# Extra matmuls behind the last product of an encoder layer: 640 with set operand places, results unread

## The chip, the cores and the metric

The kernel runs on one core of one Trainium2 chip. A core has TensorE (matrix products, called PE in the profile, with its weight loads as PEld), VectorE (DVE), ScalarE (ACT), GpSimd (POOL) and SyncE (SP), which here mostly issues DMAs. The engines run side by side and meet through semaphores. Operands of a product lie in SBUF, an on-chip memory of 128 partitions; results go to PSUM, the accumulators of TensorE, in buffers of 512 columns of four bytes. The metric is the time of one execution in microseconds, as the device measures it; lower is better.

## The reference

One step of a one-layer hybrid encoder: 1024 prompt frames and 64 frames of a running stream, width 1024. The last part is the one that the change stands behind:

```python
x = x + m                                   # m: the merged convolution and attention branches
x = x + swiglu(rmsnorm(x, g_ffn[l]), w_ff1[l], w_ff3[l], w_ff2[l])
...
return rmsnorm(x, g_final), ...

def swiglu(x, w1, w3, w2):
    return (jax.nn.silu(x @ w1) * (x @ w3)) @ w2
```

The hidden width of the feed-forward part is 2816. Besides the two normalised outputs, the step returns key and value rows and the states of the convolution.

## The kernel before

All large products run on TensorE in the type fp32r. Each float32 operand is split into a high part and a low part (`split`, line 119: ScalarE copies the high part, VectorE subtracts), and a product is made of three matmuls: high by high, high by low, low by high. A matmul `mm(out, stationary, moving)` loads 128 columns of weights (the stationary operand) and streams the moving operand, here 272 or 512 columns, past them. Products of 2 x 2 blocks are made by a scheme of seven products instead of eight (`STEPS`, line 126), with sums of blocks prepared by VectorE.

The order of work on TensorE is the order in which the code calls it: input projections and attention first, then the gates and output projection (lines 294 to 302 and 1066 to 1068), then the two upward products of the feed-forward part, written by `run` (line 218, its matmuls at line 238, 272 columns each, 24 in a group), and at last the downward product (lines 1461 to 1553).

The downward product takes 11 blocks of the hidden width, in four runs of 2, 3, 3 and 3 (`KB`, line 35). For each run, each of two groups of frames and each of the seven steps, it accumulates into a PSUM tile at line 1508, with 512 columns to a matmul. The hidden values come from HBM as the tiles `ht`. The weights of the downward product stand in rings in SBUF: `ring_of(p)` (line 1266) gives, for each of the seven steps p, one tile of 128 partitions by 4352 fp32r columns; block kp uses columns (kp mod 4) x 1024 onwards, high part first, low part 512 columns later. Columns from 4096 on hold other operands. Columns 3072 to 3583 of ring 1 also serve ScalarE as a place to throw away squares when it sums a row (line 1448).

The PSUM tiles of the downward product come from the pool `psD`: two buffers with the tag "A" and four with the tag "BD". A new tile of a tag takes the oldest buffer of that tag, and waits until its last reader is done. The reader is the add at line 1520, by which VectorE takes each product into an accumulator in SBUF.

In the last run (`final`), the last three steps are done for one frame tile after the other (line 1493). After each of them `half_ended` (line 1443) squares and sums half an output row, and when both halves are there it computes the factor, scales the halves on ScalarE (line 1456) and VectorE (line 1458), and stores them from the queues of ScalarE and SyncE (lines 1457 and 1459). The last matmul of the program is the last one of line 1508. After it only this tail runs, and then the end of the program, in which SyncE waits for every queue and engine in turn and all engines meet (line 1587).

Of the kernel before, what the change touches and what calls it, by code (L numbers as in the profile page):

```python
# [8 lines left out]
F32 = mybir.dt.float32  # L9
# [6 lines left out]
P = 128  # L16
# [48 lines left out]
def encoder_kernel(ctx: ExitStack, tc: tile.TileContext, ins, outs):  # L65
# [1396 lines left out]
    for b, ks in enumerate(blocks):  # L1462
        first, final = b == 0, b == len(blocks) - 1
        nk = blocks[b + 1] if not final else []
        for g in range(2):
# [28 lines left out]
            for si, js in turns:  # L1494
# [47 lines left out]
                if final and g == 0 and si == 4:  # L1542
# [9 lines left out]
                    vec.scalar_tensor_tensor(row, row, r[:TS], gfb[:TS], op0=ALU.mult, op1=ALU.mult)  # L1552
                    nc.sync.dma_start(outs["y_sample"], row)

_OUTS = [
    ("y_prompt", (1024, 1024), (1, 1024, 1024)),
    ("y_sample", (64, 1024), (1, 64, 1024)),
# [33 lines left out]
```

## Time and profile before

| | |
|---|---|
| time, median of two runs | 1512.9 us (1512.77 to 1513.04) |
| span of the profiled execution | 1513.8 us |
| instructions in it | 26451 |
| matmuls, weight loads | 10178 each |
| TensorE, share of the span busy with matmuls | 98% |
| VectorE, ScalarE | 65%, 45% |
| mean granted clock of TensorE | 0.994 |

The profiled execution is 0.9 us longer than the median of the timed runs. The profile gives for each engine its busy time, a picture of the span in 40 slices, groups of instructions with the line that made them, and, in time order, single instructions or runs of equal ones. In such a row come the start, the length, the engine, the line, the operation, the tiles written and read, and the count. A row whose engine ends in q is the engine's queue, which issues DMAs or waits. The chain of waits is followed back from the last instruction; its rows have start, length and what the time went to. Matmuls overlap in the array, so that the lengths of single matmuls add up to more than the time they take together; the step from one start to the next tells the pace.

### The profile page before, as it was taken

The page shows a single profiled execution, that of the slowest core. Times are in us where ns is not written, and L with a number is a line of the kernel's source. Part 1 is how long each engine was busy: PE and PEld are TensorE (multiplying, and loading weights), DVE is VectorE, ACT ScalarE, POOL GpSimd, SP SyncE. Part 2 cuts the span into 40 slices and gives each one's busy share as a digit, 9 for nine tenths or more (in the row PEclk, how much of TensorE's full clock was granted, in tenths as well). Part 3 has the DMA queues.
Part 4 walks back from the last instruction along what each step waited for, and adds up shares of the span by engine and source line. Part 5 has one row for each costly group of instructions (what it writes and reads, how often), then busy time and mean ns, then how long its engine had stood idle before and what let it go on. Part 6 is the DMA issues. An engine that isn't in the chain of part 4 may idle for free.

```text
span 1513.8 us, 26451 instructions
## 1 busy us (share of the span) xinstructions
PE 1476.9 (98%) x10178; PEld 1381.1 (91%) x10178; DVE 981.2 (65%) x1843; ACT 682.7 (45%) x1397; POOL 128.7 (9%) x236
## 2 busy tenths in 40 slices
PE   7999999999999999999999999999999999999997
PEld 5799999999999999998889999999999998788886
DVE  6886465642776752763489667666666668857576
ACT  6654433333776752542256444444444445402123
POOL 1210010001111121000100011100001011000000
PEclk9999999999999999999999999999999999999999
DMA  7597524168676529554432434443334449667675
GB/s 233 181 305 245 184 78 135 57 187 234 181 186 176 151 82 293 164 167 145 140 126 77 143 134 152 144 148 120 117 142 157 143 177 317 234 221 235 222 259 202
DMA packets 167518, 264.73 MB, mean 175 GB/s; under 512 B 19008, under 2 KB 103168, under 8 KB 167264
## 3 DMA queue, kind: packets, MB, share of 16 engines
q1 hardware_dynamic: 146736, 198.23, 42.2%
q0 software_dynamic: 19504, 62.71, 11.4%
q10 hardware_dynamic: 1152, 2.10, 0.4%
q8 instruction: 80, 1.31, 0.4%
q14 instruction: 46, 0.38, 0.1%
HBM read 171.06 MB, written 91.92 MB: 174 GB/s over the span
## 4 chain that ended last, share of the span: by engine, by line
PE 79%; DMA 8%; DVE 6%; ACT 3%; issue 3%; SPq 1%; POOL 0%; ACTq 0%; POOLq 0%; DVEq 0%
PE Aa L238 9%; PE Ab L238 9%; PE A L1508 7%; PE Da L238 4%; PE Db L238 4%; PE D L1508 3%; PE Bb L238 2%; PE Ba L238 2%; PE B L1508 2%; PE wo L1066 2%; PE wo L1068 2%; PE wo L1067 2%; PE t L903 2%; PE Ak L238 2%; PE g L300 2%
## 5 line engine op out<-in xcount | busy, mean ns | idle before, releaser
L1508 PE MATMUL A<-ring,ht 128*128 128x512 f32 x528 | 126.6, 393 | 3.6 <-ACT acc L1518 1.9
L1508 PEld LDWEIGHTS A<-ring,ht 128*128 128x128 f32 x528 | 98.8, 188 | 27.2 <-ACT acc L1518 3.2
L300 PE MATMUL g<-xn,whp 128*128 128x272 f32 x384 | 113.2, 295 | 0.0
L301 PE MATMUL g<-xn,whp 128*128 128x272 f32 x384 | 112.0, 292 | 0.0
L302 PE MATMUL g<-xn,wlp 128*128 128x272 f32 x384 | 111.6, 291 | 0.0
L121 ACT CAST ring<-w2r 128x512 fp32r<-128x512 f32 (+1 forms) x78 | 43.4, 587 | 105.7 <-PE A L1508 52.6
L121 ACT CAST hq<-sa 128x512 fp32r<-128x512 f32 x77 | 47.7, 619 | 86.4 <-DVE sa L1239 56.6
L814 DVE CUSTOM_DVE_ANT_0 p<-s,bb 128x640 f32<-128x640 f32 (+5 forms) x72 | 47.5, 661 | 45.5 <-DMA bb<-bias_d 28.6
L1227 POOL DMA_DIRECT2D h_d<-hq x77 | 40.9, 532 | 416.5 <-DVE hq L122 242.1
L122 DVE TENSOR_TENSOR hq<-sa,hq 128x512 fp32r<-128x512 f32 x77 | 53.1, 690 | 33.4 <-ACT hq L121 33.3
L300 PEld LDWEIGHTS g<-xn,whp 128*128 128x128 f32 x384 | 72.6, 189 | 1.0
L302 PEld LDWEIGHTS g<-xn,wlp 128*128 128x128 f32 x384 | 72.6, 189 | 0.5
L301 PEld LDWEIGHTS g<-xn,whp 128*128 128x128 f32 x384 | 72.7, 189 | 0.3
L1508 PE MATMUL D<-ring,ht 128*128 128x512 f32 x264 | 63.9, 393 | 1.3 <-ACT acc L1518 1.3
L122 DVE TENSOR_TENSOR wla<-rawa,wha 128x512 fp32r<-128x512 f32 x56 | 38.5, 687 | 40.5 <-ACT wha L121 40.5
L238 PE MATMUL Aa<-tt,wha 128*128 128x272 f32 x352 | 59.1, 289 | 2.5 <-ACT tt L121 2.5
L1508 PEld LDWEIGHTS D<-ring,ht 128*128 128x128 f32 x264 | 49.5, 188 | 13.1 <-ACT acc L1518 1.8
L122 DVE TENSOR_TENSOR ring<-w2r,ring 128x512 fp32r<-128x512 f32 (+1 forms) x78 | 49.0, 647 | 14.4 <-ACT ring L121 14.2
L238 PE MATMUL Ab<-mg,whb 128*128 128x272 f32 x352 | 58.4, 288 | 0.0
L238 PE MATMUL Aa<-mg,wha 128*128 128x272 f32 x352 | 58.3, 288 | 0.0
L238 PE MATMUL Ab<-tt,whb 128*128 128x272 f32 x352 | 58.2, 287 | 0.0
L121 ACT CAST wha<-rawa 128x512 fp32r<-128x512 f32 x56 | 34.8, 621 | 51.3 <-PE Ab L238 35.3
(519 smaller groups left out, 4368.2 us busy)
## 6 DMA issues: line engine op xcount, KB each, us to landing
h_d<-hq POOLq DMA_DIRECT2D x77, 512.0 KB, 3.5
ht<-h_d SPq DMA_DIRECT2D x154, 256.0 KB, 3.7
rawa<-in_w_ff SPq DMA_DIRECT2D x11, 1024.0 KB, 5.9
rawb<-in_w_ff SPq DMA_DIRECT2D x11, 1024.0 KB, 5.4
w2r<-in_w_ff SPq DMA_DIRECT2D x11, 1024.0 KB, 5.8
qd<-q_d SPq DMA_DIRECT2D x32, 272.0 KB, 4.7
rawp<-in_w_in SPq DMA_DIRECT2D x6, 1024.0 KB, 5.9
u_d<-scr SPq DMA_DIRECT2D x8, 544.0 KB, 4.6
```

Of the source, the lines that this page charges most:

```text
L121: act.copy(hi, src)
L122: vec.tensor_tensor(lo, src, hi.bitcast(F32), op=ALU.subtract)
L238: mm(t[:, j, :HN], w[:, k, :], x[p][:, l, k, j * HN : (j + 1) * HN], start=p in (1, 2, 7) and k == 0 and n == 0, stop=k == 3 and n == 2, s ...
L300: mm(out, a, p, start=k == 0, stop=False)
L301: mm(out, a, q, start=False, stop=False)
L302: mm(out, b, p, start=False, stop=k == kt - 1)
L814: vec.tensor_tensor_reduce(out=s if len(ps.shape) == 2 else s.rearrange("p (a b) -> p a b", a=2), in0=ps, in1=bias if len(ps.shape) == 2 e ...
L903: nc.tensor.transpose(tp[:, i * P : (i + 1) * P], s[:, i * P : (i + 1) * P], ident)
L1066: mm(ps, x(k, 0), wh, start=f, stop=False)
L1067: mm(ps, x(k, 0), wl, start=False, stop=False)
L1227: nc.gpsimd.dma_start(h_d[p, c - 1], hq.rearrange("p i l t -> p (i l t)").bitcast(F32))
L1508: mm(t, ht[k][:, j, x], w[:, l], start=p in (1, 2, 7) and k == 0 and n == 0, stop=k == len(ks) - 1 and n == 2, skip_group_check=p in (6, 5 ...
```

## The change

One block of code is added behind the downward product. Nothing else is touched.

```diff
+    for half in range(2):
+        pr = psD.tile([P, 512], F32, tag="A", name=f"pr{half}", bufs=2)
+        pq = psD.tile([P, 512], F32, tag="BD", name=f"pq{half}", bufs=4)
+        mv, st = ring_of(1), ring_of(2)
+
+        def some(n, count, ms, ss, banks=(0,), fresh=False):
+            for c in range(count):
+                a, b = ms[c % len(ms)], ss[c % len(ss)]
+                o = (pr, pq)[banks[c % len(banks)]]
+                mm(o[:, :n], st[:, b : b + P], mv[:, a : a + n], start=fresh or c < 2, stop=fresh or c >= count - 2,
+                   skip_group_check=True)
+
+        if half == 0:
+            for d in range(16):
+                some(272, 14, (128,), (128 + 8 * d,))
+            for d in (0, 16, 32, 64):
+                some(272, 14, (136,), (8 + d,))
+            some(272, 14, (128, 400), (128,))
+            some(272, 14, (128, 512), (128,))
+            some(272, 14, (128, 512), (128, 256))
+            some(272, 14, (128, 400), (128,), banks=(0, 1))
+            some(272, 14, (128, 512), (128,), banks=(0, 1))
+            some(272, 14, (128,), (128,), fresh=True)
+            some(272, 14, (128, 400, 2304, 2576, 128, 400), (128, 128, 128, 128, 2304, 2304), banks=(0, 1))
+            some(256, 14, (128,), (128,))
+            some(256, 14, (128,), (160,))
+            some(256, 14, (128,), (192,))
+            some(288, 14, (128,), (128,))
+            some(320, 14, (128,), (128,))
+        else:
+            for d in (0, 8, 16, 24, 32, 48, 64, 80, 96, 112):
+                some(512, 12, (128,), (128 + d,))
+            some(512, 12, (136,), (8,))
+            some(512, 12, (136,), (136,))
+            some(512, 12, (128,), (256,))
+            some(512, 12, (128, 640), (256,))
+            some(384, 12, (128,), (128,))
+            some(512, 12, (128,), (128,), fresh=True)
```

`some(n, count, ms, ss)` issues `count` matmuls of n columns. Their moving operands start at the columns `ms` of ring 1, in turn, and their weights at the columns `ss` of ring 2, in turn; both rings still hold the weights of the downward product. A set accumulates in one PSUM tile, or in two by turns where `banks` says so; with `fresh` every matmul starts its accumulation anew. Nothing reads `pr` or `pq`, and the outputs are the same as before. There are 448 matmuls in the first half and 192 in the second. Most sets keep both operands at one place throughout, and the sets differ in the distance of the two places (8 columns are 32 bytes), in whether an operand alternates between two places, and in the width.

## The prediction

> **What bounds the kernel now.** I read the head of the page first (span, busy time, granted clock), then TensorE's own rows in time order over the last 30 us, then the chain of waits for the pace of long matmul groups, and last the rows behind the final matmul.
>
> ```profile
> span 1513.8 us, 26451 instructions
> PE 1476.9 (98%) x10178; PEld 1381.1 (91%) x10178; DVE 981.2 (65%) x1843; ACT 682.7 (45%) x1397; POOL 128.7 (9%) x236
> PEclk9999999999999999999999999999999999999999
> ```
>
> TensorE is busy 98% of the span, in every slice but the first and the last, and the clock that it was granted never shows under nine tenths. So TensorE bounds the kernel. Work put behind its last matmul can be hidden by one thing alone: what the kernel still does after that matmul. The rows at the end say how much that is:
>
> ```profile
> 1501.60 2.21 PE L1508 MATMUL D<-ring,ht 128*128 128x512 f32 x9
> 1503.64 2.20 PE L1508 MATMUL A<-ring,ht 128*128 128x512 f32 x9
> ...
> 1499.92 0.67 DVE L1520 TENSOR_TENSOR acc<-A,acc 128x512 f32<-128x512 f32 x1
> 1504.37 0.68 DVE L1520 TENSOR_TENSOR acc<-D,acc 128x512 f32<-128x512 f32 x1
> 1505.98 0.68 DVE L1520 TENSOR_TENSOR acc<-A,acc 128x512 f32<-128x512 f32 x1
> 1509.01 0.75 DVE L1458 SCALAR_TENSOR_TENSOR acc<-acc,n4y,gfb 128x512 f32<-128x512 f32 x1
> 1509.79 0.33 SPq L1459 DMA_DIRECT2D out_y_prompt<-acc  x1
> ...
> L1587 POOLq EVENT_SEMAPHORE x4: 17/17/17, 1513.1 to 1513.7; - x4
> DMA to landing us min/median/max: 2.0/3.3/6.5
> ```
>
> The columns of the first rows are start, length, engine and line; the last two rows are from the views of line 1587 and of the output tensor. The last product ends at 1503.64 + 2.20 = 1505.84 us. Then VectorE adds it up, the last output half is scaled until 1509.76, its store is issued at 1509.79 and lands 2.0 to 3.3 us later, and the closing handshake of the engines runs from about 1513.1 to 1513.8. So 8.0 us of the span lie behind the last matmul, and that is all the cover there is.
>
> **The change part by part.** It removes nothing and moves nothing. It adds 640 matmuls to TensorE, behind everything that TensorE did, in program order: 448 in the first half (27 sets of 14 with 272 columns, three of 256, one of 288, one of 320) and 192 in the second (15 sets of 12 with 512 columns, one of 384). No other engine gets an instruction, no DMA is added, and no queue has anything put in front of what it did. Each matmul brings its own weight load, as each of the 10178 of before does (PEld has the same count).
>
> *Price of one.* TensorE overlaps matmuls, so the mean length in the groups (some 0.29 us for 272 columns, 0.39 for 512) is not what one costs. What it costs is the step from one start to the next, read from long unbroken groups:
>
> ```profile
> 1024.73 2.99 PE Aa L238 x24
> 1027.72 3.00 PE Da L238 x24
> 1030.72 3.01 PE Aa L238 x24
> ...
> 1340.86 4.11 PE D L1508 x18
> 1344.96 8.16 PE A L1508 x36
> 1353.12 4.09 PE B L1508 x18
> 1359.09 4.20 PE A L1508 x18
> ```
>
> These rows of the chain are start, length, count. L238 has 272 columns: 3.00 us / 24 = 125 ns. L1508 has 512: 8.16 / 36 = 227 ns in one place, 4.20 / 18 = 233 ns in another. Shape, type and line are the same there, and only the tiles differ, so the place of the operands is worth about 3% here. Single steps spread further:
>
> ```profile
> 341.78 0.29 PE L300 MATMUL g<-xn,whp 128*128 128x272 f32 x1
> 341.91 0.30 PE L301 MATMUL g<-xn,whp 128*128 128x272 f32 x1
> 342.05 0.28 PE L302 MATMUL g<-xn,wlp 128*128 128x272 f32 x1
> 342.17 0.28 PE L300 MATMUL g<-xn,whp 128*128 128x272 f32 x1
> ...
> 764.99 0.40 PE L1067 MATMUL wo<-wol,mg 128*128 128x512 f32 x1
> 766.14 0.40 PE L1066 MATMUL wo<-woh,mg 128*128 128x512 f32 x1
> 766.38 0.39 PE L1067 MATMUL wo<-wol,mg 128*128 128x512 f32 x1
> 769.85 0.39 PE L1067 MATMUL wo<-wol,mg 128*128 128x512 f32 x1
> ...
> 475.10 0.31 PE L856 MATMUL s<-kd,qd 128*128 128x320 f32 x1
> 475.68 0.49 PE L903 MATMUL t<-ident,p 128*128 128x128 f32 x3
> ```
>
> A 272-column step is 0.14 us (341.91 to 342.05) or 0.12 (342.05 to 342.17), and a 512-column one up to 0.24 (766.14 to 766.38). Between 764.99 and 769.85 lie 21 steps of 512, 231 ns each. Between 475.10 and 475.68 lie four of 320 columns, 145 ns each.
>
> I take 125 ns for 272 columns: three groups in different tiles agree within 1%, and 27 sets of different places should average as those do. For 512 columns I take 231 ns, between 227 and 233 and equal to the third place. From these two the slope is (231 - 125) / 240 = 0.442 ns a column. That gives estimates of 118 ns for 256 columns, 132 for 288 and 174 for 384; 320 has its own 145.
>
> The sum:
> - 272 columns: 378 x 125 ns = 47.3 us
> - 256: 42 x 118 = 5.0; 288: 14 x 132 = 1.8; 320: 14 x 145 = 2.0
> - 512: 180 x 231 = 41.6; 384: 12 x 174 = 2.1
> - together 99.8 us
>
> *Bounds.* With every set at the slow steps (140 ns and 240 ns, the rest 13 ns dearer in the first half and 10 in the second) the sum is 52.9 + 43.2 + 12.0 = 108.1 us. With every set at the slope alone (120 ns for 272, 226 for 512, the others likewise) it is 45.4 + 40.7 + 10.5 = 96.6.
>
> *A rule weighed.* The rows show 125 ns at 272 columns and 227 to 233 at 512. The Trainium skill, "TensorE: Matmul & The Clock Gate", section "Back-to-back issue gap", gives a warm gap of columns / 2.4 plus 2.5 ns, so 116 and 216 ns; by it the sum would be an estimate of 92.8 us and the time about 1598.7. The trace disagrees by 9 and by 11 to 17 ns a matmul, and the trace decides here.
>
> *Waits.* The new accumulators take over PSUM buffers of the last products, so a matmul could wait for VectorE. The first one takes the buffer of the A product before the last, whose last add starts at 1499.92; the second one's kind is read for the last time by 1504.37 + 0.68 = 1505.05. Both are done before TensorE is free at 1505.84. The second half's accumulator waits for the add of 1505.98, done at 1506.66; that half begins 58 us later. I price all three at nothing. If an add were late, TensorE would stand for its 0.7 us. The columns of the ring that ScalarE's squares still write (3072 to 3583) are read by no new matmul.
>
> *The end.* New matmuls follow at the pace of their predecessors, so the last one ends at 1505.84 + 99.8 = 1605.6 us. The old tail (until 1513.8) lies under the first 8 us of them and costs nothing any more. What is late next is TensorE itself; behind it comes only the closing handshake. SyncE waits there for each engine in turn. It took at least 0.7 us (from 1513.1), and at most 2.0 if the last store landed after its least 2.0 us at 1511.8. I take 1.0, near the row that shows it, so the span is 1606.6. The median of the runs, 1512.9, lies 0.9 under the profiled span of 1513.8; I carry that over: 1605.7 us, 92.8 more than before, 6.1%.
>
> **The rivals.**
>
> *The places lock into collisions.* In the kernel before, both operands' places change from matmul to matmul, so a slow step (140 ns, 240 ns) is soon followed by a fast one. A set of the change repeats one pair of places 12 or 14 times; a bad pair would be paid each time. Against it: groups with one kind of place held 233 ns for 18 matmuls and never 240. For it: nothing in the trace repeats the same moving columns at 272 or 512 wide. All sets bad gives 108.1 us and 1614.0; I give it 0.08, since place is worth 6 ns at 512 columns (227 against 233) and nothing forbids 13. The same Trainium skill page, section "Step-by-step: what each phase is for", says that loading the next weights takes no SBUF read bandwidth from the running matmul, since there are two ports. By that, places would not matter; the trace, 227 against 233 ns, does not agree with so flat a rule.
>
> *Repeated operands go at the bare slope.* If what lies above the slope is paid for changing operands, sets that repeat them cost 96.6 us, and the time is 1602.5. Unchanged weights alone do not save it: L238 uses each weight block for two or four matmuls in a row and pays 125 ns. Chance 0.06. The gap that the Trainium skill states, weighed above, would go further the same way.
>
> *The clock falls or the matmuls stop overlapping.* After an idle stretch this kernel shows what the slow clock costs:
>
> ```profile
> 810.82 1.11 PE L238 MATMUL Bb<-mg,whb 128*128 128x272 f32 x4
> 811.73 0.66 PE L238 MATMUL Bb<-mg,wlb 128*128 128x272 f32 x2
> ...
> 1330.00:1500.00 170.00, 170.00 (x749) 1.00 0.71 232
> 1506.00:1513.80 7.80, 0.00 (x0) 0.75 0.36 137
> ```
>
> Four matmuls took 0.91 us, 227 ns each instead of 125. The window rows give length, busy time (count), granted clock and DMA: 1.00 while TensorE works, 0.75 once it is idle. At 227 / 125 of the price the sum is 181 us and the time 1687. TensorE has no gap in front of the new work, so the clock has no reason to fall: 0.03.
>
> *Not slower.* The results are unread; if the program did not keep these matmuls, or kept them under the 8 us tail, the time would stay 1512.9. Within 2% means at most 30.3 us more: 640 matmuls would have to cost under 60 ns each with the tail's 8 us, less than half the 125 ns of a row. All 640 stand in the built program behind the last product, each with its wide output, and even TensorE's idle 36.9 us (1513.8 - 1476.9), if all were filled, would leave 63 of the 99.8. That the change does nothing gets 0.01.
>
> **How the numbers follow.** The forecast holds 0.82 and gives 1605.7; locked collisions 0.08 (1614), bare slope 0.06 (1602.5), slow clock 0.03 (1687), nothing done 0.01 (1512.9). The range takes in the bounds of the pace, 1602.5 to 1614.0. It goes on by 1 us above for a longer closing, and by 2.5 below for a shorter closing (0.3) and for the 68 matmuls whose width has no row of its own (some 30 ns each is 2 us): 1600 to 1615. Slow clock and nothing done stay outside. About 2% is what a measurement tells from no change: slower 0.99, same 0.01, faster 0.
>
> **What would show it right or wrong.** The page of the changed kernel should have 10818 matmuls and as many weight loads, and every other engine as before. A new line with 640 matmuls should start within 0.3 us of the last L1508 one and run without a gap for about 100 us; the last two of 40 slices should be TensorE alone, with the clock at nine tenths or more. Its 272-column sets should step at 120 to 130 ns, those of 512 at 226 to 235. The chain should end on TensorE, with about 1 us behind it. A gap in front, a set far above its neighbours, or a clock under 0.9 would prove a step wrong.

## The result and the profile after

The changed kernel took 1609.0 us (two runs, 1607.15 and 1610.85) against 1512.9 us: a ratio of 1.0623, 95% interval 1.0587 to 1.0658. It is slower by 6%, as forecast (1605.7), and inside the range.

The page of the changed kernel begins with the span, TensorE's busy time and, among the 40 slices (now 40 us each), TensorE, VectorE and the granted clock:

```profile
span 1605.1 us, 27731 instructions
PE 1574.2 (98%) x10818; PEld 1469.9 (92%) x10818; DVE 982.2 (61%) x1843; ACT 683.6 (43%) x1397; POOL 128.7 (8%) x236
PE   7999999999999999999999999999999999999999
DVE  6885465616777527635886666666666875767400
PEclk9999999999999999999999999999999999999999
```

There are 640 more matmuls and as many weight loads; VectorE, ScalarE and GpSimd have the counts of before. The last two slices are TensorE alone, at full clock. In order of time, TensorE's rows around the new work (start, length, count) are these. The gap holds 41 rows with the other 55 matmuls; the last row covers several widths and carries the form of its first matmul:

```profile
1501.91 2.20 PE L1508 MATMUL A<-ring,ht 128*128 128x512 f32 x9
1503.95 40.79 PE L1564 MATMUL pr<-ring,ring 128*128 128x272 f32 x323
...
1551.49 52.60 PE L1564 MATMUL pr<-ring,ring 128*128 128x256 f32 x262
```

The last old product ends at 1501.91 + 2.20 = 1504.11; the first new one has started 0.16 us before, since matmuls overlap. The last one ends at 1551.49 + 52.60 = 1604.09. So the new work moves TensorE's end by 100.0 us, and 1.0 us of the span lies behind it. Cut at the second half (the second window stops at 1604.00, 0.09 us short of the last end), the windows (length, busy time of TensorE, weight loads, VectorE, ScalarE, GpSimd, then clock, DMA share, GB/s) are:

```profile
1503.95:1560.39 56.44, 56.44 (x450) 56.44 (x448) 3.43 (x11) 2.60 (x8) 0.00 (x0) 1.00 0.06 22
1560.39:1604.00 43.61, 43.61 (x194) 35.74 (x192) 0.00 (x0) 0.00 (x0) 0.00 (x0) 1.00 0.00 0
```

The rows of SyncE's waits from 1500 us on say what the change cost the kernel, since SyncE ends the program (waited in total, times, longest):

```profile
SPq L1626 <- PE pr L1564: 93.0, 1, 93.0
SPq L1626 <- DMA out_y_prompt<-acc: 2.1, 2, 1.7
```

In the kernel before, SyncE's longest wait at that point is this one, and it has none for a matmul:

```profile
SPq L1587 <- DMA out_y_prompt<-acc: 2.3, 3, 1.7
```

Now SyncE waits for the last stores much as before, and then 93.0 us for TensorE. That wait ends with TensorE at 1604.1, so it began about 1511.1, which is 7.0 us behind the last old product.

### The profile page after: what moved, and what is told of

Read it like the earlier page. It is cut to its first block, busy times and chain, and to the rows that moved or that the text cites. A ratio compares the mean times of both kernels' runs of the same rounds, so it can differ in the third digit from the quotient of the medians.

```text
span 1605.1 us, 27731 instructions
## 1 busy us (share of the span) xinstructions
PE 1574.2 (98%) x10818; PEld 1469.9 (92%) x10818; DVE 982.2 (61%) x1843; ACT 683.6 (43%) x1397; POOL 128.7 (8%) x236
## 4 chain that ended last, share of the span: by engine, by line
PE 63%; issue 25%; DMA 4%; DVE 3%; POOL 2%; ACT 2%; SPq 1%; POOLq 0%; ACTq 0%; DVEq 0%
PE A L1508 7%; PE pr L1564 6%; PE Ab L238 5%; PE Aa L238 5%; PE D L1508 3%; PE Db L238 3%; PE Da L238 2%; PE B L1508 2%; PE t L903 2%; PE Ak L238 2%; PE Acc L238 1%; PE Acb L238 1%; PE Ach L238 1%; PE g L300 1%; PE g L301 1%
## 5 line engine op out<-in xcount | busy, mean ns | idle before, releaser
L1564 PE MATMUL pr<-ring,ring 128*128 128x272 f32 (+5 forms) x619 | 100.1, 320 | 0.0
L1564 PEld LDWEIGHTS pr<-ring,ring 128*128 128x128 f32 x619 | 91.0, 188 | 7.6
L121 ACT CAST hq<-sa 128x512 fp32r<-128x512 f32 x77 | 47.7, 619 | 87.1 <-DVE sa L1239 56.4
```

The lines of the kernel that those rows point to most:

```text
L121: act.copy(hi, src)
L1564: mm(o[:, :n], st[:, b : b + P], mv[:, a : a + n], start=fresh or c < 2, stop=fresh or c >= count - 2, skip_group_check=True)
```

## The experiments

The first two tell apart whether TensorE's end decides or whether each matmul is paid from the first. Line 1560 is the new line there. Nothing else is left out or changed in these two kernels.

**26 matmuls.**

```diff
-    for half in range(2):
-...
+    pr = psD.tile([P, 512], F32, tag="A", name="pr", bufs=2)
+    mv, st = ring_of(1), ring_of(2)
+
+    def some(n, count, a, b, m=P):
+        for c in range(count):
+            mm(pr[:m, :n], st[:, b : b + m], mv[:, a : a + n], start=c < 2, stop=c >= count - 2, skip_group_check=True)
+
+    some(512, 26, 128, 192)
```

> The added block is replaced by one set of 26 matmuls of 512 columns, both operands at one place each (moving at column 128 of ring 1, weights at column 192 of ring 2). Theory (TensorE's end decides, the old tail covers what fits beneath it): 26 x 227 ns = 5.9 us, TensorE ends about 1511.7 on the old clock, before SyncE gets to wait for it near 1512.8, so the time is that of before, within 0.3%. Rival (the matmuls disturb the tail, or every one is paid from the first): 5.9 us more, 0.4%.

Measured: ratio 1.0009, interval 0.9992 to 1.0026: no difference, though TensorE works 6 us longer; the rival's 0.4% lies outside the interval. SyncE's waits from 1508 us on hold no wait for `pr`.

**62 matmuls.** The last line is `some(512, 62, 128, 192)`.

> The same with 62 matmuls: 62 x 227 ns = 14.1 us. Theory: TensorE ends 14.1 us behind the last product, about 8.0 us of it lie beneath the old tail and about 1.0 us of closing comes behind, so about 7.1 us more than before (0.47%). Rival (every matmul paid from the first): 14.1 us more (0.93%).

Measured: ratio 1.0048, interval 1.003 to 1.0066, which is 7.3 us (4.5 to 10.0); 14.1 us would be 1.0093. The trace of this kernel, TensorE's row and SyncE's wait:

```profile
1503.98 14.21 PE L1560 MATMUL pr<-ring,ring 128*128 128x512 f32 x62
...
SPq L1596 <- PE pr L1560: 7.1, 1, 7.1
```

Half of the 14.1 us lies beneath the tail, and the other half is SyncE's wait. The rival is out.

**The change again, with more runs.**

> The changed kernel once more, against before, in more rounds, because two runs of each leave the size of the step open. Theory (matmuls cost their step, the tail covers 8.0 us of them, 1.0 us of closing follows): 99.8 - 8.0 + 1.0 = 92.8 us more than the median of before on the same chip, a ratio of 1.061. Rival (the 96.1 us that the two runs showed are the true size, so some 3 us come from a cost that the sum leaves out): a ratio of 1.0635.

Measured: 1608.6 us against 1515.6 us (17 runs of before, from 1511.4 to 1519.3), ratio 1.0614, interval 1.059 to 1.0638: 93.0 us between the medians. The theory's 1.061 lies in the middle of the interval, the rival's 1.0635 just inside its upper edge, so the times alone favour the theory and don't rule the rival out. The trace leaves it little room: in this profile too SyncE waits 93.0 us for `pr`, and TensorE's end moves by the 100.0 us that the sum has as 99.8.

**The same matmuls ahead of the last run of the downward product.**

```diff
         nk = blocks[b + 1] if not final else []
+        if final:
+            for half in range(2):
+                pr = psD.tile([P, 512], F32, tag="A", name=f"pr{half}", bufs=2)
+...
```

> The same 640 matmuls, put ahead of the last of the four runs of the downward product instead of behind it. Theory: no tail lies beside them there, and the old tail and closing stay at the end, so the time grows by the whole 99.8 us, 7.0 us more than with the changed kernel (0.43%); VectorE, ScalarE and the DMAs, which get 100 us ahead, win nothing back, since TensorE bounds what follows without a gap. Rival (the other engines use the time to clear waits of TensorE in the last run, or the cover was not there): the same time as the changed kernel, within 2 us, or below it.

Measured: 1614.3 us, ratio 1.0653, interval 1.0634 to 1.0672. That is 5.8 us above the changed kernel by the medians, where 7.0 was expected; the profiled spans are 1614.3 and 1607.6. TensorE's last row and the last row of VectorE:

```profile
1604.12 2.20 PE L1547 MATMUL A<-ring,ht 128*128 128x512 f32 x9
...
1609.49 0.75 DVE L1458 SCALAR_TENSOR_TENSOR acc<-acc,n4y,gfb 128x512 f32<-128x512 f32 x1
```

TensorE ends at 1606.32 and the span at 1614.3: the old tail of 8.0 us is back behind it, uncovered. The rival is out: the fastest of the five runs (1613.4) lies above the slowest of the changed kernel (1613.0). The two intervals just overlap, so the runs don't settle the size (5.8 or 7.0). The trace does: the added matmuls take 100.0 us (1444.15 to 1544.13), and from the first product of the last run to TensorE's end it is 1606.32 - 1544.13 = 62.2 us, as in the kernel before (1505.84 - 1443.65). So nothing was won back, and the whole difference is the tail of 8.0 us in place of the closing of 1.0.

The kernels of the next two experiments and of the last two ran once each, at granted clocks of 0.996 to 0.998. What they show is read from the starts of matmuls in that one trace.

**Long sets at many distances.** The change has 12 or 14 matmuls to a set, too few to see every set settle. The edit is shown against the kernel with 26 matmuls.

```diff
-    some(512, 26, 128, 192)
+    for n in (512, 272):
+        for d in (64, 72, 80, 88, 96, 104, 112, 120):
+            some(n, 40, 128, 128 + d)
```

> The added block is replaced by 16 long sets of 40 matmuls with both operands fixed: moving at column 128, weights at 192, 200, 208, 216, 224, 232, 240, 248; first 512 columns wide, then 272. Theory (the distance of the two places, by 64 columns or 256 bytes, sets a settled pace, small against the whole): after some ten steps each set settles; 512 wide at 227 for distance 64, about 233 for 72, 80, 88 and 104, 232 for 96 and 120, 229 for 112; 272 wide at 124 to 127; sum 320 x 231 + 320 x 126 = 114 us, span about 1621. Rival (bad places lock into collisions): at least one set stays at 240 or more at 512, or 135 or more at 272, for all 40 steps. Rival (history, not place): the settled pace of a set depends on the set ahead of it and neighbours do not differ.

The rows of the sets, in order; the step is the difference of two neighbouring starts, divided by 40. The first three are 512 wide at distances 64, 72 and 80, then come 104 and 112, the row behind them is distance 120, and the last five are 272 wide at 64, 72, 80, 88 and 96:

```profile
1507.70 9.24 PE L1560 MATMUL pr<-ring,ring 128*128 128x512 f32 x40
1516.77 9.49 PE L1560 MATMUL pr<-ring,ring 128*128 128x512 f32 x40
1526.10 9.50 PE L1560 MATMUL pr<-ring,ring 128*128 128x512 f32 x40
...
1554.08 9.50 PE L1560 MATMUL pr<-ring,ring 128*128 128x512 f32 x40
1563.41 9.33 PE L1560 MATMUL pr<-ring,ring 128*128 128x512 f32 x40
1572.59 9.49 PE L1560 MATMUL pr<-ring,ring 128*128 128x512 f32 x40
1581.91 5.17 PE L1560 MATMUL pr<-ring,ring 128*128 128x272 f32 x40
1586.92 5.22 PE L1560 MATMUL pr<-ring,ring 128*128 128x272 f32 x40
1591.98 5.10 PE L1560 MATMUL pr<-ring,ring 128*128 128x272 f32 x40
1596.92 5.13 PE L1560 MATMUL pr<-ring,ring 128*128 128x272 f32 x40
1601.89 5.22 PE L1560 MATMUL pr<-ring,ring 128*128 128x272 f32 x40
```

At 512 columns distance 64 steps by (1516.77 - 1507.70) / 40 = 227 ns and distance 72 by (1526.10 - 1516.77) / 40 = 233. At 272, distance 80 steps by (1596.92 - 1591.98) / 40 = 123.5 ns and distance 72 by 126.5. No set stays at 240 or 135: collisions don't lock. Neighbours differ, so place does count, and by 3% at most. What is cheap at one width isn't at the other. The paces came as expected within about 1 ns, and the span was 1623.2 us where about 1621 was.

**Fewer weight columns.** With 96, 64 or 32 weight columns, only so many rows of the product are computed. These lines stand in place of `some(512, 26, 128, 192)`.

```diff
+    for b in (192, 144):
+        for m in (128, 96, 64, 32):
+            some(512, 40, 128, b, m)
+    for a, b in ((136, 200), (136, 152), (144, 208), (144, 160)):
+        some(512, 40, a, b)
```

> The added block is replaced by 12 sets of 40 matmuls of 512 columns. Sets 1 to 4: moving at 128, weights at 192 (distance 64), with 128, 96, 64 and 32 weight columns; sets 5 to 8: the same with weights at 144 (distance 16); sets 9 to 12: 128 weight columns, moving and weights at (136, 200), (136, 152), (144, 208), (144, 160). Theory (the weight load of the next matmul and the moving stream get into each other's way in reading SBUF): at distance 64 all four at 227; at distance 16 the pace falls from 233 with 128 weight columns towards 227 with 32, by about 1.6 ns per 32 columns; and what counts is the distance, so sets 9 and 11 settle at 227, 10 and 12 at 233. Rival (the place of the moving operand alone decides): the number of weight columns changes nothing at distance 16, and sets 9 and 10 agree, as do 11 and 12.

The rows: distance 64 with 128, 96, 64 and 32 weight columns, distance 16 with the same, and the last four:

```profile
1507.45 9.23 PE L1560 MATMUL pr<-ring,ring 128*128 128x512 f32 x40
1516.53 9.37 PE L1560 MATMUL pr<-ring,ring 128*96 128x512 f32 x40
1525.73 9.35 PE L1560 MATMUL pr<-ring,ring 128*64 128x512 f32 x40
1534.92 9.43 PE L1560 MATMUL pr<-ring,ring 128*32 128x512 f32 x40
1544.19 9.49 PE L1560 MATMUL pr<-ring,ring 128*128 128x512 f32 x40
1553.52 9.30 PE L1560 MATMUL pr<-ring,ring 128*96 128x512 f32 x40
1562.66 9.47 PE L1560 MATMUL pr<-ring,ring 128*64 128x512 f32 x40
1571.96 9.43 PE L1560 MATMUL pr<-ring,ring 128*32 128x512 f32 x40
1581.23 9.28 PE L1560 MATMUL pr<-ring,ring 128*128 128x512 f32 x40
1590.35 9.50 PE L1560 MATMUL pr<-ring,ring 128*128 128x512 f32 x40
1599.68 9.28 PE L1560 MATMUL pr<-ring,ring 128*128 128x512 f32 x40
1608.80 9.49 PE L1560 MATMUL pr<-ring,ring 128*128 128x512 f32 x40
```

The part on distance holds: with the moving operand 32 and 64 bytes further on, the sets at distance 64 take 9.28 us and those at 16 take 9.50 and 9.49, so it is the distance that counts, not the place of one operand. (Weights at column 200 step by (1590.35 - 1581.23) / 40 = 228 ns here, with the moving operand at 136, and stepped by 233 above, with it at 128.) The part on the weight load falls. At distance 64 fewer weights make a set slower (9.23 to 9.43), at distance 16 they go 9.49, 9.30, 9.47, 9.43. With 32 weight columns both distances take 9.43. That fits a distance that counts through the weight load, but it is one pair of distances, and a shorter load is no cheaper; how the load acts is not shown.

**32 bytes of padding in the kernel before.** Nothing is added to TensorE.

```diff
     tpool = ctx.enter_context(tc.tile_pool(name="tpool", bufs=1, reuse_waits="tile"))
+    vec.memset(tpool.tile([P, 8], F32, name="pad"), 0.0)
```

> The kernel before with 32 bytes put ahead of the tiles of the pool that holds the rings of the steps 6, 7 and 5, so that these rings stand at the same distance to the tiles of hidden values (by 256 bytes) as the rings of the steps 1 to 4; no matmul is added. Theory (distance sets the pace): the 396 matmuls of 512 columns of these steps go from 233 to 227 ns, 2.6 us less; the 1584 matmuls of 272 columns that read the same place in the upward products move too, from 124.5 to about 125.5 ns, up to 1.6 us more; the time falls by about 1 us, which a measurement can hardly tell from nothing, and the trace shows the steps. Rival (these rings are slower for another reason, such as the side of SBUF that they stand on): the steps stay at 233 ns.

Measured: ratio 1.0003, interval 0.9991 to 1.0015. Rows of its chain of waits, downward product first:

```profile
1360.71 4.08 PE A L1509 x18
1364.80 4.08 PE D L1509 x18
...
1002.66 3.01 PE Db L238 x24
1020.70 3.01 PE Aa L238 x24
```

The groups that took 4.20 us before take 4.08 (227 ns a step), and groups of the upward product that took 2.99 take 3.01. Both moved as the distance says, and the rival is out. From its first matmul to its last the downward product takes 1505.47 - 1267.08 = 238.4 us, against 1505.84 - 1264.34 = 241.5 before. The time shows nothing: an expected gain of about 1 us lies inside the interval, which goes from 1.4 us less to 2.3 more. That the gain and the loss in the upward products cancel is worked out from the steps and not seen in the time. It is no better kernel.

**Operands of two bytes.** VectorE copies 2048 columns of each ring into a bf16 tile `two` (`raw` in the code), and the sets read that tile; four sets in fp32r stand ahead. The lines that make the copy and define `some` with 40 matmuls to a set are left out here.

```diff
+...
+    for n in (512, 272):
+        for d in (64, 80):
+            some(ring_of(1), ring_of(2), n, 128, 128 + d)
+    for n in (512, 272):
+        for d in (0, 32, 64, 16):
+            some(raw, raw, n, 128, 2304 + d)
```

> The added block is replaced by 12 sets of 40 matmuls: four in fp32r as in the change (512 columns at the distances 64 and 80, 272 at the same), then eight in bf16, operands copied to a tile of their own, 512 and 272 columns at distances of 0, 64, 128 and 32 bytes. Theory (what lies above columns / 2.4 GHz, 13 to 20 ns, comes from reading two operands of four bytes an element from SBUF at once): in bf16 the step falls to 214 to 217 ns at 512 and 114 to 117 at 272, and the distance no longer matters. Rival (it is a cost of each matmul with its weight load, whatever the type): 227 to 233 and 123 to 127 as in fp32r.

```profile
1505.30 9.23 PE L1563 MATMUL pr<-ring,ring 128*128 128x512 f32 x40
1514.36 9.49 PE L1563 MATMUL pr<-ring,ring 128*128 128x512 f32 x40
...
1542.28 8.80 PE L1563 MATMUL pr<-two 128*128 128x512 bf16 x40
1550.92 8.80 PE L1563 MATMUL pr<-two 128*128 128x512 bf16 x40
1559.55 8.80 PE L1563 MATMUL pr<-two 128*128 128x512 bf16 x40
...
1572.82 4.80 PE L1563 MATMUL pr<-two 128*128 128x272 bf16 x40
1577.45 4.80 PE L1563 MATMUL pr<-two 128*128 128x272 bf16 x40
```

In bf16 the step is (1550.92 - 1542.28) / 40 = 216 ns at 512 columns and (1577.45 - 1572.82) / 40 = 116 ns at 272, and all eight bf16 sets step at one of the two, at every distance. So the theory's numbers hold and the rival is out. By the formula that the Trainium skill gives for the gap of a single warm matmul ("TensorE: Matmul & The Clock Gate", section "Back-to-back issue gap"), columns / 2.4 plus 2.5 ns, an estimate is 215.8 and 115.8 ns: this run, in which each matmul has its own weight load, agrees with that formula in bf16, while fp32r lies 11 to 17 and 8 to 11 ns above.

**Every second element.** The copy is the same, and the lines that make it and define `some` are left out again.

```diff
+...
+    for b in (192, 208):
+        some(ring_of(1), ring_of(2), 128, b)
+    some(ring_of(1), ring_of(2), 128, 192, 2, 1)
+    some(ring_of(1), ring_of(2), 128, 192, 1, 2)
+    for x, y in ((1, 1), (2, 1), (1, 2), (2, 2)):
+        some(raw, raw, 128, 2304, x, y)
+    some(raw, raw, 128, 2336, 2, 2)
```

Here x and y are the steps, in elements, of the moving operand and of the weights.

> The added block is replaced by nine sets of 40 matmuls of 512 columns: four in fp32r (distances 64 and 80; then distance 64 with every second column as moving operand; then with every second column as weights), five in bf16 (both operands dense; moving operand every second element; weights every second element; both; both at another distance). Theory (the bytes that the two streams reach over in SBUF make what lies above 216 ns and the dependence on the place): bf16 at every second element spans the bytes of fp32r, so it goes to 227 ns or more with the moving operand spread, and depends on the distance with both spread; fp32r spread goes above 233. Rival (the type fp32r itself costs it, by the way TensorE takes its elements in): bf16 stays at 216 ns in all five sets, and fp32r keeps to 227 to 233.

```profile
1505.49 9.23 PE L1563 MATMUL pr<-ring,ring 128*128 128x512 f32 x40
1514.55 9.49 PE L1563 MATMUL pr<-ring,ring 128*128 128x512 f32 x40
1523.88 18.21 PE L1563 MATMUL pr<-ring,ring 128*128 128x512 f32 x40
1541.92 9.51 PE L1563 MATMUL pr<-ring,ring 128*128 128x512 f32 x40
1551.27 8.81 PE L1563 MATMUL pr<-two 128*128 128x512 bf16 x40
1559.92 9.19 PE L1563 MATMUL pr<-two 128*128 128x512 bf16 x40
1568.95 8.79 PE L1563 MATMUL pr<-two 128*128 128x512 bf16 x40
1577.58 9.16 PE L1563 MATMUL pr<-two 128*128 128x512 bf16 x40
1586.58 9.23 PE L1563 MATMUL pr<-two 128*128 128x512 bf16 x40
```

With the moving operand spread, bf16 goes from 216 to (1568.95 - 1559.92) / 40 = 226 ns, and fp32r from 227 to (1541.92 - 1523.88) / 40 = 451 ns. Spread weights alone leave bf16 at (1577.58 - 1568.95) / 40 = 216 and cost fp32r 7 ns. So what fits is the bytes that the moving stream passes over: 512 x 4 in 226 or 227 ns and 512 x 8 in 451 are each 9.0 to 9.1 bytes a ns and partition. This rate is not the whole price, since 272 x 4 bytes in 123.5 ns, the best pace at 272 columns, are 8.8. The rival is out. Of the theory's details, bf16 came to 226 and not 227, the second distance moved it by some 2 ns only, and fp32r with spread weights stayed at 234.

## Why the prediction was right

- **TensorE bounds, and the tail is the only cover.** Shown by 26, 62 and 640 matmuls: nothing, 7.1 and 93.0 us of SyncE's wait, where TensorE worked 5.9, 14.1 and 100.0 us longer. A matmul costs nothing until TensorE passes the point at which SyncE would have gone on, some 7 us behind the old end, and its whole step after it.
- **Price of one.** The first half was priced at 47.3 + 5.0 + 1.8 + 2.0 = 56.1 us and took 56.4; the second at 43.7 and took 43.6. The step was taken from long groups, not from the length of single matmuls, which would have doubled the sum. The 272-column sets took (1551.49 - 1503.95) / 378 = 125.8 ns where 125 was taken. That 231 fitted the 512-column sets is in part luck: it was taken between 227 and 233, and the change's distances happen to spread over just that stretch.
- **Waits at nothing.** TensorE's row runs on without a gap, so no accumulator was waited for.
- **Closing, 1.0 us.** 1605.1 - 1604.1 = 1.0.
- **The sum.** 92.8 us was predicted over the kernel before; with more runs on one chip it is 93.0 between the medians. By the interval it is 89 to 97, so the close match is luck as a time; as a trace it is 100.0 for 99.8.
- **What was off: carrying the profile's span over to the time.** The prediction took 0.9 us off the span, since the median of two runs lay that much under it. Where one execution of the changed kernel has both, the time is above the span: 1607.15 against 1605.1, and 1610.85 against 1608.7, some 2.1 us each, and in all other runs it is 2.05 to 2.18. The 0.9 came from holding one execution's span against other executions' times, and before's 19 runs on another chip spread from 1511.8 to 1521.0. By the 2.1 the profiled execution of before took about 1515.9 us, 3.0 above the median of the two runs and close to the 1515.5 and 1515.6 of the larger samples, and the forecast's span of 1606.6 would have been 1608.7, 0.3 from the measured median. The 3 us between 96.1 and 93.0 are then most likely the spread of the runs, not a cost of the change.
- **The rivals.** Collisions don't lock: no set of 40 with dense operands stood above 234 ns or 127. The bare slope is nearly reached at 512 columns at the best distance (227 against 226) but not at 272 (123.5 at best, against 120), and since sets that repeat their operands step by 227 at one distance and 233 at another, repeating is not what decides. The clock was 1.00 through the new work. The matmuls were executed.

The reason for the step's size was left open by the prediction ("the place is worth about 3%"). The runs show that in bf16 the step falls to 216 ns and the place no longer counts, that bf16 steps like fp32r (226 ns) once its moving operand is spread over as many bytes, and that in fp32r the distance of moving operand and weights adds up to 3%. That reading the moving operand at about 9.1 bytes a ns sets the fp32r step is the account that fits these runs; it was not seen directly. Whether the distance acts through the weight load stays open, and so does why 96 weight columns are cheaper than 64 at one distance and dearer than 128 at the other.

## What to carry to other kernels

Work behind the last instruction of the bounding engine is free only as long as the tail behind it; find what the closing engine waits for last, and price the rest at start-to-start steps of unbroken groups of the same shape and type. Hold a profiled span against that execution's own time, and treat the median of two runs as uncertain by the spread of many. For fp32r matmuls, the distance of the two operands by 256 bytes can be tried when padding is free (here it moved the steps and not the time); count every stage that shares the moved tiles, since a gain in one can be a loss in another.

## What the hardware showed that was not expected

- fp32r steps at 227 ns for 512 columns at best, bf16 at 216; a moving operand at every second fp32r column takes 451. Dense fp32r, spread fp32r and bf16 with its moving operand spread all come to 9.0 to 9.1 bytes a ns and partition; dense bf16 comes to 4.7.
- At 512 columns the distance of the operands sets the pace: 227 ns at 64, 233 at 72 and 80, 229 at 112 ((1572.59 - 1563.41) / 40). It appears to repeat by 64 columns of four bytes: sets at the distances 16 and 80 both take 9.49 to 9.50 us.
- Fewer weight columns can make a matmul slower: 32 instead of 128 at the best distance cost (1544.19 - 1534.92) / 40 = 232 ns against 227.
